# A hybrid attention and recurrence layer: causal mask and sum broadcast on TensorE, exponentials in two pieces, the last inverses coupled beside attention

## The chip, the cores and the metric

The kernel runs on one core of a Trainium2 chip. The metric is the device time of one execution in microseconds (us); the median of three runs is compared. A core has five engines with a queue each, worked off in order: TensorE (PE, matmuls; its weight loads have a row of their own, PEld), VectorE (DVE), ScalarE (ACT), GpSimd (POOL) and SyncE (SP, which here only issues DMAs). DMAs run beside the engines; SP, ACT and POOL issue them.

## The reference

One layer of a streaming encoder, for 2048 tokens of width 1024, all in float32:

```
u   = rmsnorm(x)
fox = forgetting_attention(u)        8 heads of 64, causal, with a cumulative log forget gate as bias
rk  = rwkv7(u)                       8 heads of 64, a recurrence with a matrix state per head
h   = x + rmsnorm_post(concat(fox, rk) @ w_out)
out = h + rmsnorm_post'(SwiGLU(rmsnorm_pre'(h)))
```

For a head the attention is softmax(q k^T / 8 + c_t - c_s) v over s <= t, where c is the running sum of the log forget gates. The recurrence is computed in chunks of 64 tokens; each chunk of each head needs the inverse of a unit triangular 64 x 64 matrix.

## The kernel before, in words

The program is written in three parts, and each engine's queue is fixed when it is built. Several generators ("lanes") are woven by `weave` (lines 86 to 114): each lane has a number of steps and a weight, the lane with the smallest weighted share done takes the next step, and the order in which steps are written is their priority. A framework then places the instructions of each engine by that priority and a simulated timeline, assigns the buffers of each tile pool and adds all semaphores.

**Stage A** (`phase_a`, line 155) projects the tokens in 4 blocks of 512, every float32 product being made from three matmuls of split operands (`mm3`). For each half block (8 in all) `stage_pre` prepares the recurrence's operands and writes 32 matrices to the DRAM tile `nd`; beside the next half block's projections `stage_solve` (446) inverts their two diagonal 32 x 32 blocks by 31 steps on DVE, stores the inverses to `td` in DRAM through POOL's queue (474 to 476), and then couples them: it loads `Q` (the off-diagonal blocks, 463), `T1` and `T2` (the inverses, 478 to 484), transposes `T1` on PE (489), and makes the off-diagonal blocks of the inverse by twice 64 matmuls of 32 x 32 (497, 505), copied by ACT and stored to `td` (508). The eighth half block's solve and coupling run last, beside the last attention projections (568). Attention's operands go to DRAM as `qS`, `kS`, `vS`, the gates as `nc`.

**Stage B** (`phase_b`, 1130) weaves three lanes: the recurrence (`rwkv`, 571; weight 0.92), the loading of the output weights, and attention (`attention`, 819; 736 steps).

The recurrence works in 32 groups of two chunks for four heads; its steps stand in `ORDER` (37). After each 4 groups (a half block) two `post_norm` follow (733), as the "tail" steps `n1`, `n2`, `n3`: DVE makes means (743), POOL subtracts them (745), ACT squares (747), DVE sums (748) and takes the inverse root, POOL multiplies (751), PE transposes (756), and PE and DVE apply the gate (764 to 766). `load_bv` (649) is a DMA of POOL's queue. One PSUM pool of two banks, `rw`, serves all its products (617).

Attention goes through 8 heads; a head has 8 units (J = 7 down to 0) of two blocks of 128 queries. `scores` (870) runs one unit ahead of `values` (915). For each query block and each 512 keys PE makes `S` from two matmuls (892, 893); DVE adds the gate bias `ng` and takes the row maximum in one instruction (900) into a row buffer `P` (4 buffers of 2048 columns). The last 128 keys of a block, where the causal mask applies, are a piece of their own: their bias `ngm` is `ng` plus the triangle `tri`, summed by POOL (877). When a block's row is complete DVE makes the maximum (905) and ACT one exponential over the whole row with its sum into `ls` (906).

At the end of a unit's scores DVE takes the reciprocal `rl` (909, one value per query, queries in partitions). It is needed along the columns of a 64-row block: POOL's queue writes it to the DRAM tile `rd` (911) and, when that has landed, reads it back broadcast to 64 partitions as `rb` (913):

```
rd = dr.tile([NQ, 128], F32, tag="rd", name="rd")
nc.gpsimd.dma_start(out=rd.rearrange("q p -> p q"), in_=rl)
u.rb = p2.tile([64, QB], F32, tag="rb", name="rb", bufs=3)
nc.gpsimd.dma_start(out=u.rb, in_=rd.rearrange("q p -> (q p)").partition_broadcast(64))
```

`values` transposes `P` on PE (935), ACT copies the transposes as `th` (941), DVE makes the rest `tl` for the longer units (943), and PE accumulates `O` (953), two pairs of key blocks later, in a PSUM pool of one buffer. `O`'s two halves are added by ACT (958) and DVE (959) into `ot`. One unit later `finish` (961) multiplies by `rb` on POOL and stores to `mixT` in DRAM from POOL's queue (962, 963).

**Stage C** is the output projection (`Mix.passes`, 1048; matmuls named `eps`) from `mixT`, its norms, and the feed-forward part. The diff does not touch it. Its first loads (1043) need the last unit of attention and the first tokens of the recurrence's output.

## Time and profile before

| what | us |
|---|---|
| median of 3 runs (3388.7 to 3393.86) | 3389.72 |
| the profiled execution, its own time | 3382.06 |
| its span, first to last instruction | 3380.3 |
| PE busy (share of the span) | 3011.6 (89%) |
| DVE busy | 2429.8 (72%) |
| ACT busy | 1533.9 (45%) |
| POOL busy | 1504.6 (45%) |

Mean granted clock of PE over the span: 0.950 of full speed, which is 2.4 GHz; the lower of its two levels is 1.2 GHz, so a stretch at 0.77 spent part of its time at each. In rows of the profile "L745" is line 745 of the kernel, `out<-in` are its tiles (a trailing number is left out: `A` is the recurrence's `A5`, `R` its `R3`, `T` is `T1` or `T2`, and `X` is `X1` or `X2`), "xN" a count, and what stands in brackets or behind an arrow is what ended the idle time of the engine before the instruction. A name such as POOLq or SPq is the issuing of DMAs. Busy time of PE includes the tail of each matmul in the pipeline, so a matmul of 0.28 us can have its successor 0.11 us behind it.

### The profile page before, as it was taken

How to read it: one execution, taken by the hardware profiler on the slowest of the kernel's cores; microseconds unless marked ns; L12 is line 12 of the kernel's file. 1: busy time of each engine (PE TensorE's matmuls, PEld its weight loads, DVE VectorE, ACT ScalarE, POOL GpSimd, SP SyncE). 2: the span in 40 equal slices, each digit the busy share in tenths (PEclk: the TensorE clock that was granted, in tenths of full speed). 3: DMA queues.
4: the chain of work that ended last, by engine and by line, in shares of the span. 5: the costliest groups of instructions: out<-in, count | busy, mean ns of one | idle time of the engine just before them, and what ended most of it. 6: DMA issues, size and time to landing. Idle time of an engine off the chain costs nothing. (4 is left out here: it accounts for less than half of the span.)

```text
span 3380.3 us, 48573 instructions
## 1 busy us (share of the span) xinstructions
PE 3011.6 (89%) x16657; PEld 2488.3 (74%) x16657; DVE 2429.8 (72%) x5249; ACT 1533.9 (45%) x2950; POOL 1504.6 (45%) x1223
## 2 busy tenths in 40 slices
PE   7999999995988899888798789999899999996895
PEld 5777777774887788878676568878788887774674
DVE  6876667663676667766635677777865556999898
ACT  5444434432766666666534433333433334333432
POOL 3354544442233323333234443443633336887776
PEclk9999999998999999999899889999999999998898
DMA  4766665668355665554168833443222224221321
GB/s 133 188 165 164 176 171 153 161 174 228 87 105 97 116 107 107 104 103 86 30 203 255 261 103 125 134 134 125 100 100 87 75 75 180 100 92 71 137 100 75
DMA packets 467723, 438.32 MB, mean 130 GB/s; under 512 B 141220, under 2 KB 382934, under 8 KB 465430
## 3 DMA queue, kind: packets, MB, share of 16 engines
q1 hardware_dynamic: 432262, 390.52, 41.7%
q0 software_dynamic: 11008, 24.20, 2.8%
q10 hardware_dynamic: 24208, 20.52, 2.0%
q8 instruction: 132, 2.16, 0.3%
q14 instruction: 113, 0.93, 0.1%
HBM read 308.31 MB, written 126.81 MB: 129 GB/s over the span
## 5 line engine op out<-in xcount | busy, mean ns | idle before, releaser
L218 POOL TENSOR_TENSOR wl<-wraw,wh 128x1024 fp32r<-128x1024 f32 (+1 forms) x108 | 264.7, 2454 | 287.9 <-ACT wh L217 265.1
L1210 POOL TENSOR_TENSOR wl<-fraw,wh 128x512 fp32r<-128x512 f32 x132 | 184.1, 1395 | 459.1 <-ACT wh L1206 446.1
L1455 POOL TENSOR_TENSOR dop<-draw,dop 128x512 fp32r<-128x512 f32 x210 | 329.9, 1601 | 104.1 <-ACT dop L1453 57.1
L1206 ACT CAST wh<-fraw 128x512 fp32r<-128x512 f32 x308 | 187.1, 618 | 377.1 <-PE gp L77 193.2
L76 PE MATMUL mm<-uh,wh 128*128 128x512 f32 (+1 forms) x864 | 346.5, 402 | 1.6 <-DVE ol L522 1.6
L77 PE MATMUL mm<-ul,wh 128*128 128x512 f32 (+1 forms) x864 | 344.5, 399 | 0.0
L78 PE MATMUL mm<-uh,wl 128*128 128x512 f32 (+1 forms) x864 | 344.2, 398 | 0.0
L76 PE MATMUL dps<-dop 128*128 128x512 f32 x624 | 249.9, 408 | 65.1 <-ACT acc L1550 28.2
L1453 ACT CAST dop<-draw 128x512 fp32r<-128x512 f32 x280 | 155.6, 620 | 236.0 <-DVE draw L1461 164.0
L77 PE MATMUL dps<-dop 128*128 128x512 f32 x624 | 247.5, 398 | 1.4 <-POOL dop L1455 1.4
L78 PE MATMUL dps<-dop 128*128 128x512 f32 x624 | 245.3, 397 | 1.2 <-POOL dop L1455 1.2
L913 POOL DMA_DIRECT2D rb<-rd x64 | 35.1, 548 | 474.0 <-DMA rd<-rl 442.2
L76 PE MATMUL gp<-za,wh 128*128 128x512 f32 x528 | 211.1, 400 | 22.8 <-ACT za L1206 17.0
L1210 DVE TENSOR_TENSOR wl<-fraw,wh 128x512 fp32r<-128x512 f32 x176 | 157.8, 897 | 81.5 <-ACT wh L1206 77.5
L77 PE MATMUL gp<-za,wh 128*128 128x512 f32 x528 | 209.5, 397 | 5.3 <-DVE za L1210 5.3
L78 PE MATMUL gp<-za,wl 128*128 128x512 f32 x528 | 209.8, 397 | 0.0
L943 DVE TENSOR_TENSOR tl<-pt,th 128x512 fp32r<-128x512 f32 (+2 forms) x280 | 162.1, 592 | 60.2 <-ACT th L941 55.8
L76 PEld LDWEIGHTS dps<-dop 128*128 128x128 f32 x624 | 120.0, 193 | 111.4 <-DVE acc L1553 36.5
L1461 DVE TENSOR_TENSOR draw<-draw 128x512 f32<-128x512 f32 x160 | 196.0, 1242 | 6.5 <-POOL dop L1455 6.0
L900 DVE CUSTOM_DVE_ANT_0 P<-S,ng 128x512 f32<-128x512 f32 (+3 forms) x288 | 167.8, 596 | 41.2 <-DMA scr_td<-X 32.4
L76 PEld LDWEIGHTS mm<-uh,wh 128*128 128x128 f32 (+1 forms) x864 | 164.5, 190 | 43.5 <-issue 4.3
L953 PE MATMUL O<-th,Vs 128*128 128x256 f32 (+1 forms) x672 | 179.8, 321 | 15.7 <-DVE ot L959 14.5
(362 smaller groups left out, 8571.7 us busy)
## 6 DMA issues: line engine op xcount, KB each, us to landing
wraw<-in_w_in SPq DMA_DIRECT2D x104, 512.0 KB
fraw<-in_ffn_w_gate SPq DMA_DIRECT2D x22, 1024.0 KB
fraw<-in_ffn_w_up SPq DMA_DIRECT2D x22, 1024.0 KB
scr_hid<-s SPq DMA_DIRECT2D x22, 1024.0 KB
draw<-scr_hid SPq DMA_DIRECT2D x22, 1024.0 KB
draw<-in_ffn_w_down SPq DMA_DIRECT2D x22, 1024.0 KB
scr_a<-A SPq DMA_DIRECT2D x16, 1280.0 KB
A<-scr_a SPq DMA_DIRECT2D x64, 320.0 KB
```

Of the source, the lines that this page charges most:

```text
L76: nc.tensor.matmul(out, lhsT=wh, rhs=xh, start=first, stop=False)
L77: nc.tensor.matmul(out, lhsT=wh, rhs=xl, start=False, stop=False)
L78: nc.tensor.matmul(out, lhsT=wl, rhs=xh, start=False, stop=last)
L218: nc.gpsimd.tensor_tensor(wl[:, :, 0:m], raw[:, :, 0:m], wh[:, :, 0:m], op=ALU.subtract)
L900: nc.vector.tensor_tensor_reduce(out=P[:, c0 + a:c0 + e], in0=S[:, a:e], in1=bias, op0=ALU.add, op1=ALU.max, scale=1.0, scalar=-3.0e38, ac ...
L943: nc.vector.tensor_tensor(tl[:, w[0], w[1]], pt[:, w[0], w[1]], th[:, w[0], w[1]], op=ALU.subtract)
L953: nc.tensor.matmul(O[:, q0 * 128:QB], lhsT=vv, rhs=p[:, e, q0:NQ, :], start=kb == 0 and i == 0, stop=kb == nkb - 1 and i == len(parts) - 1)
L1206: f.nc.scalar.copy(h, x)
L1210: e.tensor_tensor(l[:, c], x[:, c], h[:, c], op=ALU.subtract)
L1453: f.nc.scalar.copy(r[0][p][i], x)
L1455: e.tensor_tensor(r[1][p][i], x, r[0][p][i], op=ALU.subtract)
L1461: V.tensor_tensor(o[p], x[p], y[p], op=op)
```

## The change

1. `couple`, a generator of its own, holds what `stage_solve` did behind its store, with the `Q` loads moved to its start. For seven half blocks it is chained behind the solve in stage A as before; for the eighth it becomes a lane of stage B (`left`: 6 empty steps, then 4, weight 0.1), in a `P` buffer of attention and the recurrence's PSUM banks. The pool of `nd` now lives until the end.
2. The causal mask: a third matmul, identity times triangle, adds the triangle to the last 128 columns of `S`; DVE's pass over the last 512 keys becomes one instruction; `ngm` is gone.
3. The exponential of a row is made in two pieces, split at about half its 128-key blocks, each with its own sum; DVE adds the two.
4. `rl` stays in SBUF. At the end of `values` PE transposes it, broadcast to 64 columns, into `R`, the other half of `O`'s PSUM bank; ACT copies `R` to `rb`; the product and the store follow at once. `rd`, the two DMAs and `finish` are gone.
5. The recurrence's weight in stage B goes from 0.92 to 0.85.

```diff
-NSOLVE = CL // 2 + 4
+HC = CL // 2
+NSOLVE = HC
+NCOUPLE = 4
...
+def couple(k, nc, nd, td, t, bank):
+
+    t = t.rearrange("p (i a s) -> p i a s", a=NCB, s=HC)
+    Q, T1, T2, T1T, X1, X2 = (t[:, i] for i in range(6))
+    T1, T1T = (x.rearrange("p (i c) s -> p i c s", i=2) for x in (T1, T1T))
+    for g in range(4):
+        rows = slice(g * 32, (g + 1) * 32)
+        nc.sync.dma_start(out=Q[rows], in_=nd[g * NCB:(g + 1) * NCB, 0:HC, HC:CL].rearrange("c s t -> s c t"))
+        for i in range(2):
+            nc.sync.dma_start(out=T1[rows, i], in_=td[g + 4 * i:32:8, 0:HC, 0:HC].rearrange("u s t -> s u t"))
+        nc.sync.dma_start(out=T2[rows], in_=td[g * NCB:(g + 1) * NCB, HC:CL, HC:CL].rearrange("c s t -> s c t"))
+    yield
...
@@ stage_solve
-            Q = pv.tile([128, NCB, HC], F32, tag="Q", name="Q")
-            for g in range(4):
-                nc.sync.dma_start(out=Q[g * 32:(g + 1) * 32], in_=nd[g * NCB:(g + 1) * NCB, 0:HC, HC:CL].rearrange("c s t -> s c t"))
...
@@ phase_a
-                solve = stage_solve(nd, scr["td"][b * 2 + half])
+                td = scr["td"][b * 2 + half]
+                solve, nsolve = stage_solve(nd, td), NSOLVE
+                if b + 1 < NB or half == 0:
+                    bank = lambda n: ps_el.tile([128, NCB * HC], F32, tag="el", name=n)
+                    solve, nsolve = chain(solve, couple_later(nd, td, bank)), NSOLVE + NCOUPLE
...
@@ attention
+    trir = cp.tile([128, 128], F32R, name="trir")
+    identr = cp.tile([128, 128], F32R, name="identr")
+    nc.scalar.copy(trir, tri)
+    nc.scalar.copy(identr, k.ident)
...
-        ngm = p2.tile([128, NQ, 128], F32, tag="ngm", name="ngm")
-        nc.gpsimd.tensor_tensor(ngm, ng[J * QB // 512][:, qo:qo + QB].rearrange("p (b c) -> p b c", c=128),
-                                tri.unsqueeze(1).broadcast_to([128, NQ, 128]), op=ALU.add)
-        ls = p2.tile([128, NQ], F32, tag="ls", name="ls")
+        ls = p2.tile([128, NQ, 2], F32, tag="ls", name="ls")
...
+                last = c0 + n == nk
+                nc.tensor.matmul(S[:, 0:n], lhsT=Q2[:, qs], rhs=hd.Ks[c0 // 512][:, 0:n], start=False, stop=not last)
+                if last:
+                    nc.tensor.matmul(S[:, n - 128:n], lhsT=identr, rhs=trir, start=False, stop=True)
+                nc.vector.tensor_tensor_reduce(out=P[:, c0:c0 + n], in0=S[:, 0:n], in1=ng[c0 // 512][:, 0:n], op0=ALU.add, op1=ALU.max,
+                                               scale=1.0, scalar=-3.0e38, accum_out=mx[:, nm:nm + 1])
...
-                    nc.scalar.activation(P[:, 0:nk], P[:, 0:nk], AF.Exp, bias=nmx, accum_out=ls[:, qi:qi + 1])
+                    mid = nk // 256 * 128
+                    if mid == 0:
+                        nc.vector.memset(ls[:, qi, 0:1], 0.0)
+                    for i, (x0, x1) in enumerate(((0, mid), (mid, nk))):
+                        if x1 > x0:
+                            nc.scalar.activation(P[:, x0:x1], P[:, x0:x1], AF.Exp, bias=nmx, accum_out=ls[:, qi, i:i + 1])
...
-        rd = dr.tile([NQ, 128], F32, tag="rd", name="rd")
-        nc.gpsimd.dma_start(out=rd.rearrange("q p -> p q"), in_=rl)
-        u.rb = p2.tile([64, QB], F32, tag="rb", name="rb", bufs=3)
-        nc.gpsimd.dma_start(out=u.rb, in_=rd.rearrange("q p -> (q p)").partition_broadcast(64))
+        u.rl = p2.tile([128, NQ], F32, tag="rl", name="rl")
+        nc.vector.tensor_tensor(u.rl, ls[:, :, 0], ls[:, :, 1], op=ALU.add)
+        nc.vector.reciprocal(u.rl, u.rl)
...
-        O = ps_o.tile([128, QB], F32, tag="O", name="O")
+        OR = ps_o.tile([128, 2 * QB], F32, tag="O", name="O")
+        O, R = OR[:, 0:QB], OR[0:64, QB:2 * QB]
...
+        for qi in range(NQ):
+            nc.tensor.transpose(R[:, qi * 128:(qi + 1) * 128], u.rl[:, qi:qi + 1].broadcast_to([128, 64]), k.ident)
...
         nc.scalar.copy(ol, O[64:128])
-        nc.vector.tensor_tensor(u.ot, O[0:64], ol, op=ALU.add)
-
-    def finish(u):
-        nc.gpsimd.tensor_tensor(u.ot, u.ot, u.rb, op=ALU.mult)
-        nc.gpsimd.dma_start(out=scr["mixT"][u.hd.h * 64:(u.hd.h + 1) * 64, u.J * QB:(u.J + 1) * QB], in_=u.ot)
+        nc.vector.tensor_tensor(ot, O[0:64], ol, op=ALU.add)
+        nc.scalar.copy(rb, R)
+        nc.gpsimd.tensor_tensor(ot, ot, rb, op=ALU.mult)
+        nc.gpsimd.dma_start(out=scr["mixT"][hd.h * 64:(hd.h + 1) * 64, J * QB:(J + 1) * QB], in_=ot)
...
@@ phase_b
+        def left():
+
+            for _ in range(6):
+                yield
+            yield from couple(k, tc.nc, nd, scr["td"][2 * NB - 1], spare()[:, 0:6 * NCB * HC],
+                              lambda n: bank(n).rearrange("p q t -> p (q t)")[:, 0:NCB * HC])
+
-        weave((recurrence([0]), NB * (8 * 10 + 13), 0.92), (weights(), n_at // 2 + NJ, 0.9), (run(), n_at))
+        weave((recurrence([0]), NB * (8 * 10 + 13), 0.85), (left(), 6 + NCOUPLE, 0.1), (weights(), n_at // 2 + NJ, 0.9), (run(), n_at))
```

## Rows read from the trace of the kernel before

**Rows 1.** Stretches: us; PE, PEld, DVE, ACT, POOL busy; PE clock; DMA share; GB/s
```profile
800.00:846.90 46.90, 11.83 (x175) 9.10 (x173) 13.37 (x47) 3.95 (x8) 4.53 (x8) 0.63 0.82 249
846.90:1667.00 820.10, 732.62 (x5538) 661.52 (x5539) 578.90 (x1991) 532.68 (x1233) 246.58 (x355) 0.95 0.50 97
1667.00:1700.40 33.40, 10.71 (x33) 7.67 (x31) 9.21 (x34) 4.13 (x10) 13.43 (x18) 0.63 0.16 34
```

**Rows 2.** Waits in 880 to 1650: us in total, times, longest us
```profile
POOL rb L913 <- DMA rd<-rl: 403.2, 54, 11.3
...
ACT ysq L747 <- POOL yg L745: 72.0, 7, 13.4
...
PE C L708 <- ACT UV L702: 57.1, 7, 11.5
...
POOL bv L651 <- DMA scr_mixT<-bv: 27.8, 8, 10.4
...
PE S L892 <- DVE mx L900: 13.7, 21, 2.2
...
PE O L953 <- DVE ot L959: 0.7, 2, 0.5
...
PE pt L935 <- ACT P L906: 0.2, 1, 0.2
```

**Rows 3.** Timelines of POOL, ACT and PE, 1055 to 1062: start, us, what, idle before
```profile
1056.05 0.56 POOL L913 DMA_DIRECT2D rb<-rd  x1 [8.38 <-DMA rd<-rl]
...
1057.90 2.05 POOL L745 TENSOR_TENSOR yg<-yg,mn 128x512 f32<-128x512 f32 x2
...
1058.99 0.63 ACT L747 ACTIVATE ysq<-yg 128x512 f32<-128x512 f32 x1 [10.51 <-POOL yg L745]
...
1060.87 1.44 PE L708 MATMUL C<-R,UV 128*128 128x128 f32 x5 [8.34 <-ACT UV L702]
```

**Rows 4.** Busy time of two neighbouring stretches of B
```profile
975.00:1050.00 75.00, 73.56 (x605) 68.17 (x605) 56.40 (x180) 50.54 (x126) 18.92 (x29) 1.00 0.60 114
1050.00:1080.00 30.00, 19.51 (x97) 16.09 (x97) 18.22 (x77) 16.60 (x30) 12.48 (x17) 0.77 0.51 72
```

**Rows 5.** Timeline of PE at 1654: matmuls of 128 columns in a stream
```profile
1654.07 0.31 PE L892 MATMUL S<-Ks,Q 128*128 128x128 f32 x1
1654.21 0.28 PE L893 MATMUL S<-Ks,Q 128*128 128x128 f32 x1
1654.32 0.28 PE L953 MATMUL O<-th,Vs 128*128 128x128 f32 x1
```

**Rows 6.** Timeline of ACT at 1660: two exponentials, 384 and 512 columns
```profile
1660.47 0.62 ACT L906 ACTIVATE P<-P,nmx 128x384 f32<-128x384 f32 x1
...
1661.08 0.71 ACT L906 ACTIVATE P<-P,nmx 128x512 f32<-128x512 f32 x1
```

**Rows 7.** Groups by line, 845 to 1700: busy us, mean ns | idle before, releasers
```profile
L958 ACT COPY ol<-O 64x256 f32<-64x256 f32 x64 | 23.6, 369 | 29.0 <-PE O L953 27.2
```

**Rows 8.** The A/B boundary: timelines of SP and PE, then busy time by stretch
```profile
829.62 0.33 SPq L852 DMA_DIRECT2D Ks<-scr_kS  x1
...
842.46 0.83 PE L489 MATMUL tp<-ident,T 128*128 128x128 f32 x2 [32.38 <-DMA T<-scr_td]
...
846.89 0.79 PE L892 MATMUL S<-Ks,Q 128*128 128x512 f32 x1 [0.49 <-ACT X L506]
...
836.00:838.00 2.00, 0.00 (x0) 0.00 (x0) 0.00 (x0) 0.00 (x0) 0.00 (x0) 0.50 0.91 282
838.00:839.00 1.00, 0.00 (x0) 0.00 (x0) 0.00 (x0) 0.00 (x0) 0.00 (x0) 0.50 0.28 53
```

**Rows 9.** Waits in 1660 to 1712, the B/C boundary
```profile
POOL rb L913 <- DMA rd<-rl: 22.6, 3, 7.7
...
ACT ysq L747 <- POOL yg L745: 11.5, 1, 11.5
...
PE yT L756 <- POOL yg L751: 5.4, 1, 5.4
```

More of the change, by code (lines that the diff above doesn't have):

```diff
@@ L152, in vectors, with phase_a @@
     nc.vector.tensor_scalar(k.onemka, k.vec2[:, V_KA:V_KA + 4], -1.0, 1.0, op0=ALU.mult, op1=ALU.add)
-def phase_a(k, tc, ins, scr):
+def couple(k, nc, nd, td, t, bank):
[9 more added lines that the diff above has]
+    yield
+    tp = bank("tp").rearrange("p (i c s) -> p i c s", i=2, s=HC)
+    for i in range(2):
+        nc.tensor.transpose(tp[:, i].rearrange("p c s -> p (c s)"), T1[:, i].rearrange("p g t -> p (g t)"), k.ident)
+    nc.scalar.copy(T1T, tp)
+    yield
+    xp = bank("xp").rearrange("p (c s) -> p c s", s=HC)
+    for c in range(NCB):
+        for g in range(4):
+            rows = slice(g * 32, (g + 1) * 32)
+            nc.tensor.matmul(xp[rows, c, :], lhsT=Q[rows, c, :], rhs=T1T[rows, c // 4, c % 4, :], start=True, stop=True)
+    nc.scalar.copy(X1, xp)
+    yield
+    yp = bank("yp").rearrange("p (c s) -> p c s", s=HC)
+    for c in range(NCB):
+        for g in range(4):
+            rows = slice(g * 32, (g + 1) * 32)
+            nc.tensor.matmul(yp[rows, c, :], lhsT=X1[rows, c, :], rhs=T2[rows, c, :], start=True, stop=True)
+    nc.scalar.copy(X2, yp)
+    for g in range(4):
+        nc.sync.dma_start(out=td[g * NCB:(g + 1) * NCB, 0:HC, HC:CL].rearrange("c s t -> s c t"), in_=X2[g * 32:(g + 1) * 32])
+    yield
+def phase_a(k, tc, ins, scr, dr):
     nc = tc.nc
@@ L555, in phase_a, with couple_later @@
         weave((stage_l(blk), 3))
-        solve = fox = iter(())
+        def couple_later(nd, td, bank):
+            yield from couple(k, nc, nd, td, spare(), bank)
+        solve, nsolve, fox = iter(()), 1, iter(())
         for b in range(NB):
@@ L560, in phase_a @@
                 nd = dr.tile([32, CL, CL], F32, tag="nd", name="nd")
-                lanes = [(chain(*(stage_pre(blk, half * 2 + pl, nd, pl) for pl in range(2))), 14), (solve, NSOLVE), (fox, 6)]
+                lanes = [(chain(*(stage_pre(blk, half * 2 + pl, nd, pl) for pl in range(2))), 14), (solve, nsolve), (fox, 6)]
                 if half == 1 and b + 1 < NB:
@@ L814, in run @@
             yield
-    return run
+    return run, bank
 def attention(k, tc, ctx, scr):
@@ L988, in run, with spare @@
             yield from woven(*lanes)
-            if i > 1:
-                finish(units[i - 2])
-        finish(units[-1])
-    return run
+    def spare():
+        return p1.tile([128, T], F32, tag="P", name="spare", bufs=4)
+    return run, spare
 class Mix:
@@ L1127, in behind, with phase_b @@
         yield
[L1130 removed]
+def phase_b(k, tc, ins, scr, mix, nd):
     T = k.T
@@ L1134, in phase_b @@
     with ExitStack() as ctx:
-        recurrence = rwkv(k, tc, ctx, ins, scr)
-        run = attention(k, tc, ctx, scr)
+        recurrence, bank = rwkv(k, tc, ctx, ins, scr)
+        run, spare = attention(k, tc, ctx, scr)
         nj = T // (NQB * 128)
@@ L1594, in fox_rwkv7_block @@
     constants(k, tc, ctx, ins)
-    phase_a(k, tc, ins, scr)
+    nd = phase_a(k, tc, ins, scr, ctx.enter_context(tc.tile_pool(name="a_dr", bufs=2, space=DRAM)))
     NB = T // BT
```

62 lines of the change are left out of this document (10 added, 52 removed).

## The prediction

> **What bounds the kernel now.** The change touches the end of the projection stage (A), the stage in which attention and recurrence run together (B), and, through B's last work, the start of the output projection (C). So I first read the table of busy time by stretch [rows 1]. In B, 846.9 to 1667, TensorE (PE) is busy for 732.62 of 820.10 us, with VectorE (DVE) at 578.90, ScalarE (ACT) at 532.68 and GpSimd (POOL) at 246.58. Before B lies a stretch of 46.9 us with 11.83 us of PE, and behind it one of 33.4 us with 10.71 us. Those two are boundaries: their length is set by a chain of waits and not by an engine's work.
>
> Then the table of waits inside B [rows 2]. POOL waits 403.2 us for the first half of a round trip through DRAM: `rl` is written to `rd` and read back, spread over 64 partitions, as `rb` (line 913). That alone would cost nothing, since POOL bounds nothing. But ACT waits 72.0 us, in 7 pieces, for POOL's line 745, and PE waits 57.1 us, in 7 pieces, for ACT's line 702. The timelines of one piece show the link [rows 3]: POOL sits 8.38 us in front of line 913, only then comes line 745 (the mean subtracted, first step of the norm behind each half block of the recurrence), ACT's line 747 has waited 10.51 us for it, and PE's line 708 has waited 8.34 us for an ACT copy queued behind line 747. One small broadcast thus stops three in-order queues, once per half block.
>
> What a stop costs is read from two neighbouring stretches [rows 4]. From 975 to 1050 PE is busy 73.56 of 75 us at full clock; here PE is the bound. From 1050 to 1080 it is busy 19.51 of 30, so 10.5 us are idle against 0.6 at the usual share: 9.9 lost. The mean granted clock is 0.77 there, so 2 x 0.23 x 30 = 13.8 us run at 1.2 instead of 2.4 GHz, and between 3.3 us (all the idle time lies in them) and 13.8 of these held work that took twice as long: 1.7 to 6.9 lost. Together 11.6 to 16.8; I take 14. (By instructions, 97 against 605 per 75 us, it would be 18, but the gate's long matmuls fall in that stretch.)
>
> **The change, part by part.**
> *Round trip gone.* Lines 908 to 913, the `ngm` sum (877) and the late `finish` go; `rl` is now turned into a row block by two PE transposes a unit and copied out by ACT. POOL's queue then holds the product `ot*rb`, its store, the `bv` loads and the norm. The 7 stops end: 7 x 14 = **-98**. Not all of it: the norm's chain DVE, POOL, ACT, DVE stays, and PE's waits for `mx`, 13.7 us in 21 pieces [rows 2], are three for each stop; I leave half of them, **+7**.
> *More for PE.* 128 mask matmuls (one per query block) and 128 transposes, each with 128 moving columns. In a stream such a matmul moves the next start by 0.14 and 0.11 us [rows 5]; 256 x 0.11 = **+28**, and since PE is the bound between the stops, I hide none of it. Bounds: 0, if all fell into gaps, and 256 x 0.3 = 77, if each stood alone for its whole duration. The Trainium skill, "TensorE: Matmul & The Clock Gate", section "Back-to-back issue gap", gives about 81 ns a matmul for a stream of weight loads and matmuls of 128 columns; by it this term would be an estimated 21 us, and the rows here stand above it.
> *More for ACT.* 120 of the 128 exponentials are cut in two. From 384 to 512 columns the exponential goes from 0.62 to 0.71 us, 0.09 for 128 columns, and the next starts 0.61 us behind the 384-column one [rows 6], so some 0.3 us of each is fixed: 36 us. 64 copies of `rb`, as large as `ol` (369 ns [rows 7]), add 24. ACT goes from 65% of B to about 78%. PE's work covers it; without that cover it is 60 us. I take **+4**, bounds 0 and 60. The two pieces let the first transposes start after half an exponential, but PE waits only 0.2 us for line 906 in all of B [rows 2], so I count no gain.
> *DVE and POOL.* 96 short score passes merge into their neighbours; 64 additions and 8 memsets of a few columns come. All lies beside PE: nothing.
> *Coupling moved.* The last inverse's transposes, 128 small matmuls, 3 copies, 16 loads (4 of `Q`, moved from ahead of the solve, and 12) and 4 stores go from the A/B boundary into B. The work took 842.46 to 846.89, 4.4 us [rows 8], and PE pays it again: **+4**. It borrows one of four `P` tiles for some 22 of 736 attention steps (a second block of scores may wait for the first to be consumed: up to 10 us), and SP has its 16 loads ahead of later query loads, which are issued two units early. In phase A the same generator only moves the `Q` loads behind the solve; the steps keep their places in the weave, so nothing.
> *A/B boundary.* PE waits 32.38 us for the `T` loads, and the first scores start at 846.89 [rows 8]. With the loads gone the next thing late is `Ks` of the first head: its last piece is issued at 829.62, with five more pieces of 256 KB behind it in the same queue, and the heavy stream runs at 282 GB/s until about 838, then falls to 53 [rows 8]. 1.3 MB at that rate is 4.6 us, so `Ks` lands near 834 and the scores start near 835: **-12**. Bounds: 0 (another load is as late as the inverses) and -17 (the load lands as it is issued).
> *B/C boundary.* In the last stretch POOL waits 22.6 us in three round trips; on the chain to the output projection ACT's wait for line 745 is 11.5 us and PE's for line 751 is 5.4 [rows 9]: 17, less about 1 that the norm keeps: **-16**, bounds -8 (half of it is taken by the attention's own last unit) and -22 (all of POOL's waits). The recurrence's weight in the weave, 0.92 to 0.85, I put at 0 here (a rival below).
>
> Sum: -98 + 7 + 28 + 4 + 4 - 12 - 16 = **-83 us**. On the profiled execution, 3382.06 us, that gives 3299; the median of the runs lies 7.7 us above it, and the forecast for the median is **3307 us**.
>
> **Rivals.**
> *Another wait in POOL's queue.* The product `ot*rb` now stands where the broadcast stood and waits for the end of a unit's values; `bv` loads wait for a store, 27.8 us in 8 pieces now [rows 2]. If one of them is regularly ahead of line 745, half of the 98 stays: +49, **3356 us**. For: the queue order is fixed and in order. Against: the `bv` loads are written two groups away from line 745, and a unit's values end within a few us of their place.
> *Recurrence too early.* With 0.85 the recurrence ends 0.07 x 736 = 52 steps sooner by the program's order, and attention runs that much longer alone: 52/736 of 820 us is 58 us in which PE has no second stream. If a third stays empty, +19: **3326 us**. Against: in the trace the recurrence does not end early at all; its last steps run beside the last unit.
> *The accumulator's bank (slower than before).* `O` has one buffer. `R` now shares it, so the next unit's first value matmul waits until ACT has copied `rb`, behind whatever stands in ACT's queue. PE waits only 0.7 us for `O` in B today [rows 2]; to eat the gain it would have to idle 83/64 = 1.3 us in every unit. At 2 us, which needs ACT to lag by five copies, the cost is 128: **3435 us**, slower. For: ACT at 78% and in order. Against: two value steps of lag and a second stream stand ahead of that matmul. The Trainium skill, "PSUM — Partial Sum Buffer", section "PSUM bank collisions raise a hardware error", asks that engines be kept apart by bank and quadrant and not by address; by that rule the copies of `ol`, `ot` and `rb` could not overlap the transposes into the same bank, which is this rival's mechanism; no row before shows it.
>
> **How the numbers follow.** Forecast as summed, 3285 to 3328 (the stop's bounds, 7 x 2.6 = 18 either way, and a few us of the boundaries): 0.62. More than that (PE packs better without stops), 3265 to 3285: 0.06. Recurrence too early: 0.13. Another POOL wait: 0.14. The bank: 0.05. The range 3275 to 3357 leaves out the bank and most of the best case. A measurement tells 0.2%, 6.8 us, from no change: all cases but the bank are faster; with a little bleeding from the POOL rival, 0.93 faster, 0.03 same, 0.04 slower.
>
> **What would show it.** Right: no wait of POOL near 8 us in B, ACT's wait at line 747 down to 1 or 2 us, PE's clock near 1.00 through B, B some 55 us shorter, the first scores near 835, and 17 us between B's last attention work and the first `eps`. Wrong: ACT still waiting at line 747 (a new owner of POOL's queue), PE waiting for `O` or for `rb`, PE far below 97% in the last 60 us of B, or a first score that still starts near 845.

## The result and the profile after

The changed kernel takes **3305.05 us** (median of four runs, 3300.75 to 3310.0) against 3391.79 (four runs, 3388.7 to 3397.72): ratio **0.974**, interval 0.972 to 0.976. The forecast was 3307. The profiled execution took 3300.75 us with a span of 3299.0; the one of before took 3382.06, so the two profiled executions differ by 81.3, and the sum of the prediction was 83.

For the comparison I cut both kernels at the same three events: the first score matmul, the last one, and the first `eps` matmul of the output projection. Before, they start at 846.89, 1660.66 and 1700.39, which gives 813.8 and 39.7 us between them; behind `eps` both kernels take 1679.9. The busy time by stretch (us; PE, PEld, DVE, ACT, POOL; PE clock; DMA share; GB/s), first before, then after the change:

```profile
846.89:1660.66 813.77, 727.55 (x5507) 657.39 (x5508) 575.40 (x1975) 527.45 (x1217) 245.32 (x353) 0.95 0.51 98
1660.66:1700.39 39.73, 15.78 (x63) 11.80 (x61) 12.70 (x51) 9.36 (x26) 14.69 (x20) 0.69 0.14 29
```

```profile
800.00:826.33 26.33, 16.25 (x97) 13.17 (x95) 13.60 (x47) 9.33 (x24) 2.64 (x4) 0.85 0.97 302
826.33:1586.38 760.05, 737.78 (x5821) 669.22 (x5822) 574.25 (x1845) 569.94 (x1496) 125.80 (x172) 0.99 0.35 103
1586.38:1619.10 32.72, 13.87 (x71) 10.79 (x69) 17.52 (x58) 13.41 (x40) 12.39 (x15) 0.76 0.36 105
1619.10:3299.00 1679.90, 1522.08 (x6464) 1224.18 (x6464) 1267.14 (x1822) 635.43 (x1110) 883.96 (x586) 0.95 0.37 125
```

So the gain is 20.6 us ahead of the first score, 53.7 between the scores and 7.0 between the last score and `eps`. PE's busy time between the scores rose from 727.6 to 737.8, in 54 us less; the clock rose from 0.95 to 0.99 [rows 1].

The waits in 880 to 1600 (us in total, times, longest), which answer to [rows 2]:

```profile
POOL ot L976 <- ACT rb L975: 408.3, 53, 15.4
POOL bv L664 <- DMA scr_mixT<-bv: 70.9, 8, 11.7
...
POOL yg L758 <- DVE mn L757: 47.0, 8, 7.0
...
DVE vr L761 <- ACT ysq L760: 4.7, 3, 3.4
...
PE O L965 <- ACT rb L975: 4.2, 6, 1.9
...
PE S L904 <- DVE mx L909: 2.2, 6, 0.4
```

POOL waits as long as before, but for its own next work, and no engine inherits it: ACT's wait for `yg` (72.0 before) has no row left, and PE's for ACT's copy of `UV` (57.1 before) is 0.9. The norm of one half block now passes while PE works, which answers to [rows 3] and [rows 4]. ACT's timeline (no idle time stands in front of either square), and the stretch around it:

```profile
1021.51 0.63 ACT L760 ACTIVATE ysq<-yg 128x512 f32<-128x512 f32 x1
...
1025.03 0.63 ACT L760 ACTIVATE ysq<-yg 128x512 f32<-128x512 f32 x1
```

```profile
1010.00:1040.00 30.00, 29.26 (x209) 25.58 (x208) 25.85 (x106) 23.66 (x67) 9.33 (x12) 1.00 0.38 112
```

PE is busy 29.26 of 30 us at full clock, where [rows 4] had 19.51 at 0.77.

The new matmuls in PE's timeline (start, duration), which answer to [rows 5]:

```profile
1577.44 0.22 PE L908 MATMUL S<-trir,identr 128*128 128x128 f32 x1
1577.50 0.33 PE L965 MATMUL O<-tl,Vs 128*128 128x256 f32 x1
...
1588.45 0.38 PE L969 MATMUL O<-ident,rl 128*64 128x128 f32 x2
1588.67 0.27 PE L947 MATMUL pt<-ident,P 128*128 128x128 f32 x1
```

A mask matmul moves the next start by 0.06 us, each transpose of `rl` by 0.11 (the medians of the 128 of each are the same): 128 x 0.06 + 128 x 0.11 = 22 us of issue, not 28. The Trainium skill, "TensorE: Matmul & The Clock Gate", section "Back-to-back issue gap", has 81 ns for this width; by it the estimate was 21, and the trace agrees with it in the mean of the two kinds, but with neither kind alone.

The A/B boundary, which answers to [rows 8]. A head has four pieces of `Ks`, loaded from the last to the first, and the first score needs the first, so the fourth of these loads. SP's issue of it before, then after the change, and PE's first score after:

```profile
823.49 1.37 SPq L852 DMA_DIRECT2D Ks<-scr_kS  x1
```

```profile
820.01 0.89 SPq L868 DMA_DIRECT2D Ks<-scr_kS  x1
```

```profile
826.33 0.80 PE L904 MATMUL S<-Ks,Q 128*128 128x512 f32 x1 [5.95 <-DMA Ks<-scr_kS]
```

`Ks` is what is late, as forecast, but 8.7 us earlier than I had put it. (The loads at 825.40 and at 829.62 before, the latter in [rows 8], are the fifth and sixth: pieces of the second head.) At the B/C boundary [rows 9]: POOL's last store of attention, SP's wait for it, the load that follows, and ACT's queue:

```profile
1606.88 0.59 POOL L977 DMA_DIRECT2D scr_mixT<-ot  x1 [0.29 <-POOL ot L976]
```

```profile
SPq L1057 <- DMA scr_mixT<-ot: 4.9, 2, 4.7
```

```profile
1605.37 0.62 SPq L1221 DMA_DIRECT2D fraw<-in_ffn_w_gate  x1
...
1613.66 0.36 SPq L1057 DMA_DIRECT2D er<-scr_mixT  x1
```

```profile
1613.57 1.14 ACT L1227 CAST wh<-fraw 128x512 fp32r<-128x512 f32 x2 [7.90 <-DMA fraw<-in_ffn_w_gate]
1617.39 1.14 ACT L1227 CAST wh<-fraw 128x512 fp32r<-128x512 f32 x2 [2.69 <-DVE fraw L1245]
1618.44 1.66 ACT L1058 CAST emh<-er 128x512 fp32r<-128x512 f32 x3
```

The recurrence's chain is gone from here; the end is now set by attention's own last store, which lands beside a weight load of 1 MB for the feed-forward stage (before, that load was issued at 1703.14, behind the first `eps`). Casts of that weight stand in ACT's queue ahead of the cast `emh` for which `eps` waits.

### The profile page after: what moved, and what is told of

The parts are those of the page before. It is cut to its first block, busy times and chain, and to the rows that moved or that the text cites. A ratio compares the mean times of both kernels' runs of the same rounds, so it can differ in the third digit from the quotient of the medians.

```text
span 3299.0 us, 48970 instructions
## 1 busy us (share of the span) xinstructions
PE 3032.2 (92%) x16913; PEld 2511.0 (76%) x16913; DVE 2434.5 (74%) x5129; ACT 1584.9 (48%) x3256; POOL 1383.9 (42%) x1031
## 5 line engine op out<-in xcount | busy, mean ns | idle before, releaser
L976 POOL TENSOR_TENSOR ot<-ot,rb 64x256 f32<-64x256 f32 x64 | 46.4, 726 | 428.2 <-ACT rb L975 428.2
L955 DVE TENSOR_TENSOR tl<-pt,th 128x512 fp32r<-128x512 f32 (+1 forms) x280 | 163.2, 591 | 73.2 <-ACT th L953 69.6
L909 DVE CUSTOM_DVE_ANT_0 P<-S,ng 128x512 f32<-128x512 f32 (+2 forms) x320 | 183.6, 605 | 24.8 <-PE pt L947 13.9
L920 ACT ACTIVATE P<-P,nmx 128x896 f32<-128x896 f32 (+7 forms) x248 | 187.5, 761 | 14.4 <-DVE nmx L914 14.1
```

Source lines behind the costliest of these rows:

```text
L909: nc.vector.tensor_tensor_reduce(out=P[:, c0:c0 + n], in0=S[:, 0:n], in1=ng[c0 // 512][:, 0:n], op0=ALU.add, op1=ALU.max, scale=1.0, scala ...
L920: nc.scalar.activation(P[:, x0:x1], P[:, x0:x1], AF.Exp, bias=nmx, accum_out=ls[:, qi, i:i + 1])
L955: nc.vector.tensor_tensor(tl[:, w[0], w[1]], pt[:, w[0], w[1]], th[:, w[0], w[1]], op=ALU.subtract)
```

## The experiments

All stage times below are cut as above, from each kernel's profiled execution. The runs e5 to e8 were made on another chip, on which the kernel before took 3431.91 us instead of 3388.65 (e1 to e4) and 3388.03 (e9 to e12), while the changed kernel's near twins took the same there as elsewhere (e5: 3305.04, e4: 3304.85); so I compare by stages and by medians, and give a ratio only beside the kernel before of the same chip. The stages are from one execution of each kernel. What follows the first `eps` is not in the table: 1679.9 us before and after, 1675.7 to 1686.9 in the other runs.

| kernel | first score at | to last score | to first `eps` | sum of both | median, us |
|---|---|---|---|---|---|
| before | 846.9 | 813.8 | 39.7 | 853.5 | 3391.79 |
| after | 826.3 | 760.1 | 32.7 | 792.8 | 3305.05 |
| e1 round trip put back | 829.7 | 851.1 | 64.4 | 915.5 | 3442.24 |
| e2 broadcast alone | 846.4 | 743.8 | 49.1 | 792.8 | 3326.58 |
| e3 coupling in A | 846.3 | 781.6 | 33.0 | 814.6 | 3344.92 |
| e4 weight load placed | 827.5 | 761.7 | 32.6 | 794.3 | 3304.85 |
| e5 weight casts later | 827.8 | 762.1 | 31.1 | 793.2 | 3305.04 |
| e6 weight 0.92 | 835.2 | 777.8 | 32.5 | 810.3 | 3326.91 |
| e7 mask by POOL | 828.6 | 760.9 | 28.6 | 789.5 | 3307.61 |
| e8 before, trip on SP | 846.0 | 930.2 | 40.7 | 970.9 | 3502.49 |
| e9 coupling in A, 0.80 | 850.8 | 759.5 | 33.7 | 793.2 | 3326.44 |
| e10 transposes twice, 0.80 | 828.6 | 779.7 | 24.6 | 804.3 | 3317.05 |
| e11 one exponential, 0.80 | 828.2 | 783.2 | 23.9 | 807.1 | 3314.91 |
| e12 mask by POOL, 0.80 | 833.1 | 780.8 | 22.6 | 803.5 | 3314.80 |

### e1 and e2: the broadcast, taken out of the change and put alone into the kernel before

e1:

```diff
+        nc.gpsimd.dma_start(out=rd.rearrange("q p -> p q"), in_=rl)
...
+        nc.gpsimd.dma_start(out=u.rb, in_=rd.rearrange("q p -> (q p)").partition_broadcast(64))
...
-            nc.tensor.transpose(R[:, qi * 128:(qi + 1) * 128], u.rl[:, qi:qi + 1].broadcast_to([128, 64]), k.ident)
...
-        nc.scalar.copy(rb, R)
```

(the product again in `finish`, a unit later). e2 is the kernel before with the reverse of this edit and nothing else.

> The changed kernel, with the DRAM round trip of the reciprocal sums and the deferred product put back as they were before; mask by TensorE, two exponentials, coupling in B and 0.85 stay. Theory (POOL's in-order queue is what the gain in B comes from): POOL shows the two waits near 8 us per unit again, the wait of ACT's square on POOL's yg returns with some 5 us a time, TensorE's granted clock in B falls from 0.99 to 0.92-0.95, and first score to last score grows from 760 to 825-850 us, since the stops (98 us) return while 128 transposes (14 us) go; in all 3370 to 3395 us. Rival 1 (the gain of B is the mask on TensorE, the exponentials or the coupling, and the round trip was hidden): first score to last score stays within 760-775, in all 3300 to 3320. Either way the first score stays near 826 us, because that part lies ahead of the round trip.

> The kernel before, with the broadcast of the reciprocal sums by TensorE alone; mask by POOL, one exponential a row, coupling in stage A and 0.92 stay. Theory: the whole gain of B and none of the A/B boundary's. First score near 847 us as before, first score to last score 745 to 770 us (before 813.8, with the change 760.0 although that has the coupling's 4 us and the mask's 8 us in it), TensorE's granted clock in B 0.98 to 1.00; in all 3318 to 3335 us. Rival 1 (parts act only together, for instance because POOL's addition of the mask, 47 us in all, stands in the same queue): first score to last score 785 us or more, in all over 3345. Of the end of B: with this part alone the stretch from the last score to the first eps matmul shrinks from 39.7 to 20-34 us if the shorter tail came from the missing round trip.

e1 gave ratio 1.015 (1.012 to 1.018), slower than the kernel before; e2 gave 0.981 (0.978 to 0.984). Waits of e1 in 880 to 1680, its DMA row in 880 to 1600 (KB each, median us from issue to landing), and the two stretches of e1 and of e2:

```profile
POOL rb L929 <- DMA rd<-rl: 405.4, 53, 11.2
...
POOL rd L927 <- DVE rl L925: 51.6, 17, 10.8
...
ACT ysq L760 <- POOL yg L758: 32.6, 6, 14.9
PE yT L769 <- POOL yg L764: 32.5, 7, 11.9
```

```profile
rd<-rl POOLq DMA_DIRECT2D x53, 1.0 KB, 9.2
```

```profile
829.71:1680.86 851.15, 743.47 (x5524) 671.93 (x5525) 559.14 (x1814) 542.49 (x1403) 202.54 (x293) 0.92 0.48 96
1680.86:1745.22 64.36, 41.54 (x241) 35.85 (x239) 23.77 (x85) 20.99 (x65) 13.60 (x19) 0.68 0.11 26
```

```profile
846.44:1590.21 743.77, 712.32 (x5467) 640.76 (x5468) 563.74 (x1949) 534.35 (x1251) 169.90 (x232) 0.99 0.35 101
1590.21:1639.27 49.06, 35.28 (x230) 30.77 (x229) 21.91 (x77) 19.32 (x57) 9.33 (x12) 0.76 0.07 19
```

With the round trip POOL's stops, ACT's and PE's waits behind them and the clock of 0.92 are back; with the broadcast alone the clock is 0.99. First score to `eps` is 792.8 in e2, the same as with the whole change: **from the first score to the first `eps` the broadcast alone gives all of the 60.7 us**, and mask, exponentials, coupling and the weight of 0.85 together neither add nor take there. (With 0.92 kept, as in e2, the first three do cost: 810.3 in e6 below.) Behind `eps` e2 takes 1686.9, 7.0 more than the change, which no run explains. The other part of the gain is the start: e2's first score stands at 846.4, as before.

I had e1 too low by 47 us against the upper end. Two things that I had not counted show. POOL waits 51.6 us for `rl` itself (4.7 before), since it now comes to the `rd` transfer ahead of DVE. And 241 PE matmuls are left behind the last score (71 after the change): the recurrence has been placed later against attention in the queues. How the 62 us by which e1's stages exceed those of the kernel before divide between the two, no run separates.

The Trainium skill, "DMA: Bandwidth & Descriptors", section "Anatomy of one DMA — SWDGE (gpsimd) path", gives some 2.0 us of fixed cost for such a transfer. The row above has 9.2 us for 1 KB; the measurement decides.

### e8: the same round trip in another queue

```diff
-        nc.gpsimd.dma_start(out=rd.rearrange("q p -> p q"), in_=rl)
+        nc.sync.dma_start(out=rd.rearrange("q p -> p q"), in_=rl)
...
-        nc.gpsimd.dma_start(out=u.rb, in_=rd.rearrange("q p -> (q p)").partition_broadcast(64))
+        nc.sync.dma_start(out=u.rb, in_=rd.rearrange("q p -> (q p)").partition_broadcast(64))
```

> The kernel before, with the two DMAs of the round trip issued on SP's queue instead of POOL's; nothing by TensorE, the rest as before. Theory (the stop is the in-order queue of POOL, not the travel of the sums): POOL's 419.6 us of waits for rd vanish from B, the wait of the square on POOL's yg (72.0 in all before) falls below 20, and last score comes 40 to 75 us sooner than before, whole 3315 to 3350; SP then waits near 8 us a unit, 420 to 500 us in all, and the query loads behind it come late by as much without stopping TensorE. Rival 1 (the travel itself decides, since the product needs rb and with it the output ot's buffer): no gain, 3380 or more. Rival 2 (SP's wait delays loads that matter, queries, keys or the recurrence's operands): the granted clock in B stays at 0.95 or lower and the whole is 3390 to 3450.

Ratio to the kernel before on the same chip: 1.021 (1.018 to 1.023). SP's wait and POOL's, 850 to 1700, and the stretch between the scores:

```profile
SPq L913 <- DMA rd<-rl: 439.7, 54, 10.2
```

```profile
POOL ot L962 <- DMA rb<-rd: 147.9, 18, 12.2
```

```profile
846.01:1776.21 930.20, 757.92 (x5507) 678.34 (x5508) 573.25 (x1975) 528.39 (x1217) 168.81 (x232) 0.90 0.41 85
```

What DVE and PE wait for in e8, 850 to 1770:

```profile
DVE rl L909 <- DMA rd<-rl: 91.2, 10, 14.9
```

```profile
PE S L892 <- DVE mx L900: 71.0, 26, 12.5
```

The first expectation failed. The same 8.1 us a unit now stand in SP's queue, and the second expectation is the nearest: no gain, and POOL still waits, now for `rb`, and ACT's square for POOL's `yg` (82.8 us, 7 times). What nobody had named is `rl` itself: DVE waits 91.2 us for the `rd` store to let go of its buffer, and PE waits 71.0 us for DVE's `mx` instead of 13.7. The third expectation has the clock right (0.90), but the whole lies above its 3450, and the loads behind the transfer, its reason, are not what PE waits for: 1.4 us for queries in all of this stretch. So the trip costs through everything that needs its data or its buffer, and here SP was the worse place. By the medians of that chip e8 is 70.6 us slower than the kernel before; the 117 us by which the stages differ compare two chips. The Trainium skill, "Trainium Kernel Development and Optimization", section "Key Constraints", says that issuing from several engines concurrently only saves issue time, since all queues run on the same DMA engines; by it moving two DMAs would change little, and this run differs: what waits for the transfer is not in that rule.

### e4 and e5: the weight load and the weight casts at the B/C boundary

e4 asks for the 1 MB load behind the mix loads of two tiles, e5 for the first weight casts behind six `emh` casts (`issue_after` orders issue on one engine and adds no wait):

```diff
...
+        with f.tc.issue_after(f.mix.ld[3].ins):
             f.wload(0)
```

```diff
...
-            yield from itertools.islice(f.wq, 1)
+            with f.tc.issue_after(f.mix.cs[5].ins):
+                next(f.wq)
+            yield
```

> The changed kernel, with one edit: the load of the first gate weight (1 MB) is issued on its queue behind the loads of the second mix tile, instead of ahead of six of those loads. Theory (the 7 us that the end of B gained instead of 16 were lost to that load and to the two weight casts on ACT that wait for it, 7.90 and 2.69 us, in front of the cast that the first eps matmul waits for): last score to first eps 32.8 us becomes 23 to 27 us, ACT's wait at the weight cast no longer stands ahead of the cast of emh, and the whole becomes 6 to 9 us shorter, 3296 to 3299 against 3305. Rival 1 (eps waits for the last store of attention and the loads of mixT themselves, the casts are only beside it): last score to first eps 30 us or more, in all within 3 us of the change. Rival 2 (the time goes again behind it, since the weight preparation is then late for the first gate product): eps starts sooner, but from eps to the end takes 1684 to 1689 us instead of 1679.9.

> The changed kernel, with one edit that does alter the order on ACT: the first weight casts of the feed-forward stage stand behind the casts of emh for the first three mix tiles, where four of them stood between the first and the second cast of emh. Theory (the 7 to 9 us that the end of B did not give are this queue): the first eps matmul starts 22 to 26 us after the last score instead of 32.7, and the whole takes 6 to 10 us less, 3295 to 3299 against 3305. Rival 1 (the loads of mixT land late in any case): 30 us or more, whole within 3 us. Rival 2 (the weight preparation is late for the first gate product): eps starts sooner, but eps to end grows from 1679.9 by as much.

e4 changed nothing and decides nothing: the load that I had named as the one to follow was ahead of the weight load already, so the order stayed, and `eps` comes at the same distance (32.6). e5 did change ACT's order: the casts of the weight are out of the way, and the wait got another name. POOL's last store, SP's load behind it and ACT's cast in e5:

```profile
1610.34 0.59 POOL L977 DMA_DIRECT2D scr_mixT<-ot  x1 [0.29 <-POOL ot L976]
```

```profile
1617.42 0.36 SPq L1058 DMA_DIRECT2D er<-scr_mixT  x1
```

```profile
1620.26 1.66 ACT L1059 CAST emh<-er 128x512 fp32r<-128x512 f32 x3 [11.11 <-DMA er<-scr_mixT]
```

The last store of attention, its landing (7.1 us until SP may issue the load) and the load (2.8 us until the cast) set the end; the first rival held, 31.1 us, whole unchanged. The orders of the other runs bear on the slow landing. The last store lands in 6.6 to 7.4 us where the 1 MB load was issued 1.5 us ahead of it (after, e4, e5, e9), in 2.6 to 4.1 where it was 2.7 to 2.9 us ahead (e10 to e12), and in 2.1 where it came behind, by 6.6 us in e7 and 9.2 before. The landing after the change and in e7, and ACT's cast in e7:

```profile
scr_mixT<-ot POOLq DMA_DIRECT2D x1, 64.0 KB, 6.7
```

```profile
scr_mixT<-ot POOLq DMA_DIRECT2D x1, 64.0 KB, 2.1
```

```profile
1617.42 1.66 ACT L1066 CAST emh<-er 128x512 fp32r<-128x512 f32 x3 [5.59 <-DMA er<-scr_mixT]
```

In e7 (its edit is below) both the weight load and its casts stand behind what the first `eps` needs. From the last score to the last store e7 and the change take the same 20.5 us, from there to `eps` 8.1 against 12.2. In e3 and e6 the load comes 4.3 to 4.8 us behind the last store, but ACT waits 10.5 and 11.3 us for it ahead of the cast of `emh`, and `eps` comes 33 us behind the last score again. So the load and its casts together seem worth some 4 us here, and each seems enough by itself to hold `eps` up. This is read from orders that other edits made: an edit that moves the load alone was not made, and e7 differs by the mask too.

### e3, e6 and e9: the coupling and the weight, and the place of the recurrence in the order

e3 leaves the last coupling in stage A, e6 sets the weight back, e9 is e3 with 0.80:

```diff
-                if b + 1 < NB or half == 0:
+                if True:
...
-        weave((recurrence([0]), NB * (8 * 10 + 13), 0.85), (left(), 6 + NCOUPLE, 0.1), (weights(), n_at // 2 + NJ, 0.9), (run(), n_at))
+        weave((recurrence([0]), NB * (8 * 10 + 13), 0.85), (weights(), n_at // 2 + NJ, 0.9), (run(), n_at))
```

```diff
-        weave((recurrence([0]), NB * (8 * 10 + 13), 0.85), ...
+        weave((recurrence([0]), NB * (8 * 10 + 13), 0.92), ...
```

> The changed kernel, with the last inverses coupled in stage A again, as before; all else as changed. Theory of the prediction (only the loads of Ks decide, so the boundary gives 12 us): first score 12 us later than the change's 826.3, near 838, and first score to last score 4 us shorter, near 756; in all some 8 us more, 3309 to 3316 (against 3305). Rival 1 (the trace after says 20.6 us came from the boundary, because the queues in front of the loads empty sooner too): first score near 845-849, first score to last score 752-760, in all 3315 to 3328. Rival 2 (the start of B comes from other parts, such as POOL's queue without the mask): first score stays within 3 us of 826.

> The changed kernel, with the weight of the recurrence's lane back at 0.92; all else as changed. Step of the prediction (the weight moves nothing, since the recurrence stays locked to the units): whole within 4 us of 3305, last score to first eps within 4 us of 32.7. Rival 1 (from the run with the broadcast alone, where 0.92 stood and 230 matmuls were left behind the last score, 71 with the change): the recurrence ends 20 to 30 us later against the last attention unit, the last score comes 10 to 16 us sooner, last score to first eps is 45 to 50 us, and the sum stays within 5 us; then the weight only moves work from the tail into B. Rival 2 (the order of the instructions, which every edit redraws, decides by itself): head period away from 95-96 us by 2 us or more, whole 3315 to 3340.

e3 gave 3344.92 (3334.26 to 3346.16), e6 3326.91 (3320.08 to 3328.73): the first beyond all that I had expected, the second as its second rival said. Both have 18 to 22 us more between the scores, which nothing in the edits asks for. The busy time over three heads (from the last store of the third, to within some us, to that of the sixth) after the change and in e3, and PE's waits in e3's three heads:

```profile
1138.00:1424.00 286.00, 280.81 (x2188) 255.10 (x2187) 219.88 (x715) 217.77 (x577) 47.11 (x66) 0.99 0.37 109
```

```profile
1161.00:1458.00 297.00, 281.94 (x2180) 255.50 (x2181) 223.15 (x723) 217.81 (x578) 46.86 (x66) 0.98 0.36 104
```

```profile
PE S L904 <- DVE mx L909: 7.7, 9, 1.3
PE C L721 <- ACT R L687: 4.2, 3, 1.4
```

The work is the same, the time 11 us more: three short waits a head for `mx` and one for `R`, repeated in every head. e6 has the same pair (8.9 and 4.2). Both kernels have the same order of PE's instructions in the middle of B, and it is not that of the change: the recurrence's `Y` of block 11 of 16 stands behind 559 of the 768 score matmuls, against 551. That suggested e9, in which the coupling stays in A and 0.80 brings the order back to 551.

> The changed kernel with the last inverses coupled in stage A again, as in the run e3, but with the recurrence's weight 0.80. Counted in the kernels' own order of TensorE's instructions, the recurrence's step of block 11 of 16 stands behind 551 of the 768 score matmuls with the change and in this kernel, and behind 559 in e3 and in e6 (weight 0.92). Theory (the 3 us a head that e3 and e6 lost are that place in the order, not the coupling and not the weight): head period 95 to 96 us as with the change (e3 and e6: 98 to 99), PE's waits for DVE mx and ACT R in three heads below 3 us together (e3: 13), first score near 846, first score to last score 752 to 764, last score to first eps 32 to 34, whole 3318 to 3330. Rival 1 (the coupling in A costs B by itself, through what it leaves in the queues): head period 98 or more, whole 3335 to 3348 as e3.

e9 gave 3326.44 (ratio 0.981, 0.980 to 0.983), and the theory held, but for a first score 5 us later than put. Its three heads and its waits:

```profile
1161.00:1447.00 286.00, 281.16 (x2179) 255.58 (x2177) 218.93 (x712) 216.37 (x573) 46.98 (x66) 0.99 0.36 108
```

```profile
PE Y L738 <- ACT th L953: 1.2, 3, 0.4
PE S L904 <- DVE mx L909: 1.1, 3, 0.4
```

First score to last score is 759.5 with the coupling in A, 760.1 with it in B: **inside B the coupling costs nothing, at the start it is worth 20 to 24 us, and a shift of the recurrence by eight score matmuls, in every second block, is worth 3 to 4 us a head.**

### e7, e10, e11 and e12: mask, transposes and exponentials

e7 puts the mask back on POOL and VectorE, e10 makes the transposes twice, e11 takes one exponential a row; e10 to e12 have the weight 0.80, e12 being e7 with that weight.

```diff
-                    nc.tensor.matmul(S[:, n - 128:n], lhsT=identr, rhs=trir, start=False, stop=True)
...
+        nc.gpsimd.tensor_tensor(ngm, ng[...], tri..., op=ALU.add)
```

```diff
-        for qi in range(NQ):
+        for qi in (0, 1, 0, 1):
             nc.tensor.transpose(R[:, qi * 128:(qi + 1) * 128], u.rl[:, qi:qi + 1].broadcast_to([128, 64]), k.ident)
```

```diff
-                    mid = nk // 256 * 128
+                    mid = 0
```

> The changed kernel, with the causal mask added by POOL on VectorE's side again (POOL makes the sum of gate row and triangle, two reductions on the last piece of a row) and no mask matmul; all else as changed. Prediction's price of the mask matmul: 128 by 0.06 to 0.11 us, so first score to last score 8 to 14 us shorter (746 to 752), whole 3291 to 3300, as far as POOL's 47 us of additions stay hidden. Rival 1 (POOL's addition stands in a queue that also carries the recurrence's products and the units' products, as the run with the broadcast undone suggests): first score to last score 765 to 780, whole 3310 to 3330. Rival 2 (VectorE's 128 extra reductions, some 0.2-0.3 us each, 25 to 40 us, come onto the path): first score to last score 775 or more with VectorE's busy time up by 25 or more.

> The changed kernel with the 128 transposes of the reciprocal sums made twice (the same values written again), and the recurrence's weight 0.80, which places the recurrence at or ahead of the change's place in the order (544 against 551 score matmuls at block 11 of 16; with 0.85 the doubled transposes would put it at 559, the place at which e3 and e6 lost 3 us a head). Theory (TensorE is the bound of B at a granted clock of 0.99, so each transpose costs its 0.11 us): first score to last score 770 to 778 (760.1 with the change), whole 3315 to 3325. Rival 1 (the transposes fit beside other waits, as the run with the mask on POOL hints, whose TensorE was 12.5 us less busy at the same length): 757 to 765, whole 3300 to 3311. Rival 2 (the place in the order, being another than the change's, costs by itself): head period 98 or more with waits of PE for DVE mx as in e3.

> The changed kernel with one exponential a row, as before, instead of two pieces; weight 0.80, which places the recurrence ahead of the change's place in the order (537 against 551 score matmuls at block 11 of 16). Price of the prediction: ACT's busy time in B falls by 30 to 40 us (fixed parts of the second pieces and their read of the sum), all of it beside TensorE, so first score to last score within 4 us of 760 and the whole within 5 us of 3305. Rival 1 (the two pieces shorten the wait of the transposes for the exponentials, and one piece brings it back): PE's wait for ACT P at the transposes appears, first score to last score 768 to 780. Rival 2 (ACT's queue carries the recurrence's copies too, so less work there shortens B): 745 to 755, whole below 3299.

> The changed kernel with the causal mask by POOL and VectorE (as in e7), and weight 0.80, which lets the recurrence end ahead of the last attention work by more. Theory (e7's TensorE had 13 us less to do, given back as waits for DVE mx and ACT R that depend on the place of the recurrence in the order): those waits fall from 8.6 us in three heads to below 4, first score to last score 748 to 756 (760.9 in e7), last score to first eps 28 to 33, whole 3292 to 3302, the best of all. Rival 1 (the waits come from VectorE's extra reductions and POOL's additions): first score to last score 759 or more, whole 3303 to 3312.

The stretches between the scores of e7, e10, e11 and e12, in this order:

```profile
828.60:1589.49 760.89, 725.25 (x5681) 651.90 (x5682) 580.62 (x2030) 567.36 (x1492) 171.55 (x236) 0.99 0.35 103
```

```profile
828.63:1608.29 779.66, 750.71 (x5941) 685.87 (x5942) 578.48 (x1876) 569.86 (x1500) 128.56 (x175) 0.98 0.35 100
```

```profile
828.18:1611.40 783.22, 746.39 (x5821) 679.93 (x5822) 580.54 (x1999) 543.43 (x1269) 129.54 (x176) 0.97 0.34 100
```

```profile
833.13:1613.96 780.83, 736.44 (x5692) 662.24 (x5693) 587.05 (x2066) 569.10 (x1501) 173.72 (x239) 0.98 0.35 100
```

e7: PE is 12.5 us less busy and the stretch is as long as after the change. The mask matmul's PE time bought nothing when it was taken away; its 13 us came back as waits (in three heads `S` for `mx` 5.4, `C` for `R` 3.2). VectorE's extra reductions (96, not the 128 of the expectation) add 6.4 us to its busy time. With the median at 3307.61 (3302.16 to 3314.71) the mask's place makes no difference that can be told.

e12 was meant to be the best and is 7 us slower than e7 by the median (on another chip; by the stages of one execution each it is 14). With 0.80 the recurrence stands at 450 of its 640 score matmuls instead of 468, its last square starts 20 us ahead of the last unit's transposes of `rl` instead of 5, attention runs alone for longer, and the two stages together cost 803.5 instead of 789.5: 20 more between the scores, 6 less behind them. e10 and e11 have the same early place (544 and 537 of 768) and the same shape, 779.7 and 783.2 between the scores, 24.6 and 23.9 behind them. That makes them poor measures of their own edits: their excess over the change, 11.5 and 14.3 us in the sum, is about the 14.0 that the weight alone cost from e7 to e12. What can be read is that one exponential instead of two takes 26.5 us of busy time from ACT and that no gain shows, and that doubling the transposes adds 12.9 us to PE's busy time between the scores, with a price somewhere from nothing to 11.5 us.

No run beat the changed kernel; e4 and e5 are level with it.

## Why the prediction was right, point by point

**Round trip gone (-98 and +7).** The mechanism held in every row: no wait of POOL for a DMA near 8 us that others inherit, no wait of ACT for `yg`, PE's waits for `mx` down from 13.7 to 2.2, the clock at 0.99, first to last score 53.7 us shorter where 55 was the sum. The split of that sum was not right. By e2 the broadcast alone is worth 60.7 us from the first score to `eps`. My terms for it were -98 + 7 + 14 for the transposes in B, and -16 at its end: -93. Of the 32 us that are missing, 7 lie between the scores (70.0 gained against 77 summed) and 25 behind them (9.3 lost against 16 gained, with 230 matmuls left there instead of 63). So the stops were priced too high, or an order that lets the recurrence fall behind ate a third; the runs do not tell the two apart.

**More for PE (+28), for ACT (+4), coupling in B (+4).** Beside the broadcast these cost nothing up to `eps` that the stages show, as long as the weight is 0.85: e2 and the change both need 792.8 us (the change 16.3 more between the scores and 16.3 less behind them, with 159 matmuls fewer left there). With 0.92 kept, mask, exponentials and coupling cost 17.5 (e6 against e2), near the 22 summed for them without the transposes: the weight, put at nothing, gave this back (through the order, see e9). The step that failed, for the kernel as it stands, is "since PE is the bound between the stops, I hide none of it". The issue cost is 22 us, but e7 gave 12.5 us of PE time back and gained nothing; PE, busy 737.8 of 760.1, still has room that the order of the queues leaves and takes. ACT's 36 us were 26.5 in e11, hidden as taken. These errors and that of the stops have opposite signs; that B's -55 came out is in part luck.

**A/B boundary (-12).** It gave 20.6, outside the bound of 17, and e9 confirms it from the other side (24.5 later with the coupling in A). The step that failed is "its last piece is issued at 829.62 ... so `Ks` lands near 834": that load is a piece of the second head. The piece that the first score needs went out at 823.49, and the bound of 17 was read from the same wrong row. After the change it goes out at 820.01, and the score starts 6.3 us behind it. The same 6.3 us behind 823.49 would have given a start near 830 (an estimate), so some 5 of the 8.6 us missed are the misread row. The other 3.5 come from the queue ahead, which I had left as it stood: a store of `vS` that SP issued ahead of the piece before (819.89) now comes behind it (821.48).

**B/C boundary (-16).** It gave 7.0. The chain that I removed is gone, but the step "17, less about 1 that the norm keeps" did not name what is late next: attention's own last store and the load behind it. My bound of -8, "half of it is taken by the attention's own last unit", was this case, and I should have taken it. e5 shows that the casts in ACT's queue are not the cause alone, and e7, where the weight load too comes later, reaches `eps` 4.1 us sooner. That the two boundary errors, 8.6 too little and 9.0 too much, cancel is luck.

**The weight (0).** "I put at 0 here" fails as a general step. e6 costs 22 us by the median against e5 on the same chip, and has, against the change, a start 9 us later and 17.7 us more between the scores. By e9 the weight works by the order that results and not by how much of the recurrence is done: 0.80 with the coupling in A gives the same order in the middle of B as 0.85 with the coupling in B.

**The rivals.** Another wait in POOL's queue: the `bv` loads' wait for a store did grow, 27.8 to 70.9, and stopped nobody. The recurrence too early did not happen at 0.85, but it is real: at 0.80 it costs 14 us by the stages and 7 by the medians (e7 to e12), against the 19 worked out. The accumulator's bank: PE waits 4.2 us for `rb` in all of 880 to 1600, 0.07 us a unit against the 1.3 from which it would decide. (Of the copies that the forecast names there, `ol` is read from partitions 64 to 127 while `R` fills 0 to 63, so only `ot` and `rb` share partitions with the transposes.)

## What to carry to other kernels

A transfer that has to be waited for is priced by all that waits with it: the queue it stands in, the product that reads it and the engine that needs its buffer back. Moving it to another queue leaves the last two, and can cost more than it saves (e8). Where a builder draws up the order of several interwoven streams, every edit redraws it, and a difference of 3 us a head may belong to the order and not to the edit; count the place of one stream against the other in both kernels before believing an ablation. At a boundary, ask of each load that stays whether it moves up too, and of each load that becomes free to start early what it will share the DMA engines with.

## What was not expected of the hardware

The kernel before took 3431.91 us (3423.67 to 3439.05, clock 0.941 to 0.946) on one chip and 3388.65 (3383.66 to 3400.6, 0.946 to 0.949) on another, 1.3% apart, while close relatives of the changed kernel, without the DRAM round trip, took 3305.04 and 3304.85. No trace of the kernel before on the slower chip was taken, so the cause stays open.

A store of 64 KB from POOL's queue landed in 6.6 to 7.4 us where a load of 1 MB had been issued 1.5 us ahead of it in SP's (four runs), and in 2.1 us where that load came 6.6 us or more behind it (e7, before).
